# One list of 19 places for weight pieces and their parts, a new order of the last experts, and a reordered tail, in a one-core decoder layer

## The chip, the cores and the metric

The kernel runs on one core of a Trainium2 chip. The metric is the device time of one execution in microseconds (us). A profiled execution also gives a span, from the first to the last instruction; all times of single instructions below come from that execution.

## The reference, cut to what matters

One decoder layer over 512 tokens of width 1024, in f32: a mixer (retention heads beside sliding-window attention), then a mixture of experts, then an embedding gate and a last norm.

```python
h = h + jnp.concatenate([ret, att], axis=-1) @ w_out[i]
h = h + moe(rmsnorm(h, g_moe_norm[i]), w_router[i], b_router[i],
            w_up[i], b_up[i], w_down[i], b_down[i])        # top 4 of 32 experts
gate = jax.nn.sigmoid(h @ w_ple_gate[i])
h = h + rmsnorm(gate * (p[i] @ w_ple_proj[i]), g_ple_norm[i])
...
return rmsnorm(h, g_final)
...
def expert_block(args):
    xblk, e = args
    h = xblk @ w_up[e] + b_up[e]                           # 1024 x 2048
    return clamped_swiglu(h) @ w_down[e] + b_down[e]       # 1024 x 1024
```

Every expert's weights are read once: 12 MB for each of 32 experts.

## The kernel before

**Stages.** The mixer runs first and ends with the out-projection (`w_out`, in four pieces) and the routing. Then the 32 experts run one after the other, and last the tail: the projection of `p` by `w_ple_proj`, the gate product `h @ w_ple_gate` for four tiles of 128 tokens (`gate`, twice 512 columns for each tile), two norms, and the output.

**Pieces.** All weights come in pieces of 1 MB, a tile of 128 x 2048 f32 named `raw`. An expert has eight pieces for its up product (`w_up_piece`, L186) and four for its down product (`w_down_piece`, L192): 384 pieces, numbered here from 0 in the order in which SyncE (SP) issues them: up of expert 0, up of 1, down of 0, up of 2, down of 1, and so on. A piece can be issued when a place is free: there are RAW1 + RAW2 + RAW3 = 3 + 5 + 4 = 12 places in one ring, so the load of piece n waits for whatever empties the place of piece n - 12. SP's queue is in order; a load that waits holds all behind it.

**Large and small experts.** Experts are sorted by their count of tokens into 18 large ones ("L", up to 96 tokens) and 14 small ones ("S", up to 64), and `BIG` says which place in the sequence takes which kind. For an L expert every piece is split into a high part `wh` by ScalarE (ACT, L150) and a low part `wl`, the rest, by VectorE (DVE, L151); these have rings of their own, three deep each. TensorE (PE) then makes three products for each block (`wh` by the high rows, `wh` by the low rows, `wl` by the high rows; L847 for up, L928 for down). The raw place is free when the split is done. An S expert uses the raw piece itself (L864), with two matmuls in the array beside each other, and holds the place until PE is done.

**Order on PE.** In code, step e of the loop makes the up product of e, then the transposes of the rows of expert e + 1 (`prep` L300 or `prep64` L815), then the down product of e - 1. A scheduler turns this into one queue for each engine; `tc.issue_after` holds a step behind another. The rows of an expert are gathered from memory by GpSimd (POOL), `xe<-xg`.

**The tail.** After the last expert, `p` is transposed, the four token tiles are projected (three ahead of, one behind, a conditional), then comes the conditional itself (L1118, L1119: a path for experts with more tokens than their slots, which isn't taken with this input), then `h2` is read back from `acc` (L1177), and the gates run tile by tile: transposes of tile i, gate products of tile i, norm of tile i.

Of the kernel before, what the change touches and what calls it, by code (L numbers as in the profile page):

```python
# [22 lines left out]
P = 128  # L23
# [13 lines left out]
RAW1, RAW2, RAW3 = 3, 5, 4  # L37
# [9 lines left out]
BIG = [c == "L" for c in "LL" + "SLSLSLSLSLSLSLL" + "SLSLSLSLSLSLLLS"]  # L47
# [48 lines left out]
def hymba_kernel(ctx, tc, x, p, positions, rel_bias_table, g_mix_norm, w_in, b_in, ret_norm_g,  # L96
# [27 lines left out]
    rawp = pool(ctx, "rawp", RAW1)  # L124
    whp = pool(ctx, "whp", 3)
    wlp = pool(ctx, "wlp", 3)
# [7 lines left out]
    R = SimpleNamespace(eid={})  # L134
    free = [rawp] * RAW1

    def raw_tile(dt=F32):
        pl_ = free.pop(0)
        return pl_.tile([P, 2048], dt, name="raw"), pl_
# [58 lines left out]

    pieces = [w_ret(0, 0), w_ret(0, 4), w_kv, w_half(w_in, 0, 2048), w_half(w_in, 4, 2048)]
# [6 lines left out]
    for e in range(1, E + 1):  # L206
        if e < E:
            pieces += [w_up_piece(e, k) for k in range(8)]
        pieces += [w_down_piece(e - 1, f) for f in range(4)]
    n_moe = len(pieces)  # L210
# [6 lines left out]
    def prefetch(after=None):  # L217
        if free and state["next"] < min(len(pieces), state["limit"]):
            t, pl_ = raw_tile()
# [3 lines left out]
            queue.append((t, pl_))  # L223
            state["next"] += 1

    def next_piece(parts=None, dst=None, more=True):
        t, pl_ = queue.pop(0)
        r = split(t, parts, dst)
        free.append(pl_)
# [3 lines left out]

    def whole_piece(use):

        t, pl_ = queue.pop(0)
        use(t)
        free.append(pl_)
        prefetch()
# [87 lines left out]
    raw3 = pool(ctx, "raw3", RAW3)  # L327
    mix = [raw3.tile([P, 2048], F32R, name="raw").rearrange("p (a k t) -> a p k t", a=2, k=KD) for _ in range(NT)]
# [6 lines left out]
    p1 = px.enter_context(ExitStack())  # L335
    actp = pool(p1, "actp")
# [9 lines left out]
    prefetch()  # L346
    nc.sync.dma_start(out=xts[1], in_=x_v[:, 1, :])
    prefetch()
# [267 lines left out]
    raw2 = pool(right, "raw2", RAW2, side="right")  # L616
    rt = pool(right, "rt", side="right")
    free += [raw2] * RAW2
# [11 lines left out]
    b_hi = whp.tile([P, 2048], F32R, name="wh")  # L630
# [647 lines left out]
```

## Time and profile before

| what | value |
|---|---|
| time, median of 3 runs | 1489.59 us (1488.67 to 1491.34) |
| the profiled execution's own time | 1492.54 us |
| its span | 1490.8 us |
| TensorE busy in the span | 1359.1 us (91%) |
| VectorE, ScalarE, GpSimd busy | 826.1, 680.5, 222.7 us |
| mean granted TensorE clock | 0.952 of full speed (2.4 GHz) |
| bytes moved by DMA | 462.47 MB, 310 GB/s over the span |

The profiled execution is 2.95 us longer than the median, and 1.74 us of its time lie outside the span. Busy shares over the whole span mix a mixer, an expert stage and a tail that have different limits, so the rows further down are taken by stage.

### The profile page before, as it was taken

How to read it: one execution, taken by the hardware profiler on the slowest of the kernel's cores; microseconds unless marked ns; L12 is line 12 of the kernel's file. 1: busy time of each engine (PE TensorE's matmuls, PEld its weight loads, DVE VectorE, ACT ScalarE, POOL GpSimd, SP SyncE). 2: the span in 40 equal slices, each digit the busy share in tenths (PEclk: the TensorE clock that was granted, in tenths of full speed). 3: DMA queues.
4: the chain of work that ended last, by engine and by line, in shares of the span. 5: the costliest groups of instructions: out<-in, count | busy, mean ns of one | idle time of the engine just before them, and what ended most of it. 6: DMA issues, size and time to landing. Idle time of an engine off the chain costs nothing. (4 is left out here: it accounts for less than half of the span.)

```text
span 1490.8 us, 16875 instructions
## 1 busy us (share of the span) xinstructions
PE 1359.1 (91%) x6090; PEld 912.4 (61%) x6091; DVE 826.1 (55%) x1012; ACT 680.5 (46%) x756; POOL 222.7 (15%) x238
## 2 busy tenths in 40 slices
PE   5998999778999999999999999999999999999885
PEld 4776777566666474656556657474655647675564
DVE  6635674777456273545537647363544627683356
ACT  5332543545446253434526536353443625573443
POOL 1213132465010000001000000000100000000023
PEclk9997999879999999999999999999999999999998
DMA  8431027678799999999999999999999999987521
GB/s 264 124 101 57 3 107 287 226 261 315 254 408 391 409 396 394 408 397 403 387 389 407 397 389 387 383 403 392 391 396 396 392 387 401 396 325 289 172 79 45
DMA packets 110427, 462.47 MB, mean 310 GB/s; under 512 B 10830, under 2 KB 29180, under 8 KB 77568
## 3 DMA queue, kind: packets, MB, share of 16 engines
q1 hardware_dynamic: 99584, 436.24, 74.6%
q0 software_dynamic: 10320, 24.52, 6.5%
q8 instruction: 49, 0.80, 0.2%
q10 hardware_dynamic: 432, 0.57, 0.1%
q14 instruction: 42, 0.34, 0.1%
HBM read 447.26 MB, written 18.73 MB: 313 GB/s over the span
## 5 line engine op out<-in xcount | busy, mean ns | idle before, releaser
L151 DVE TENSOR_TENSOR wl<-raw,wh 128x2048 fp32r<-128x2048 f32 (+2 forms) x243 | 530.5, 2223 | 154.1 <-ACT wh L150 150.6
L150 ACT ACTIVATE wh<-raw 128x2048 fp32r<-128x2048 f32 (+2 forms) x243 | 442.9, 1858 | 111.3 <-PE up L847 56.1
L864 PE MATMUL up<-raw,xTh 128*64 128x512 f32 x896 | 195.4, 594 | 0.0
L896 DVE TENSOR_SCALAR a<-up 128x512 f32<-128x512 f32 x50 | 32.9, 687 | 265.9 <-ACT sg L895 265.9
L847 PE MATMUL up<-wh,xTh 128*128 128x512 f32 x576 | 162.5, 404 | 9.2 <-ACT wh L150 7.8
L847 PE MATMUL up<-wl,xTh 128*128 128x512 f32 x576 | 160.7, 401 | 2.2 <-DVE wl L151 2.2
L895 ACT ACTIVATE sg<-up 128x512 f32<-128x512 f32 x50 | 27.9, 594 | 295.1 <-issue 158.5
L847 PE MATMUL up<-wh,xTl 128*128 128x512 f32 x576 | 160.7, 401 | 0.9 <-DVE xTl L292 0.9
L864 PEld LDWEIGHTS up<-raw,xTh 128*64 128x64 f32 x896 | 63.1, 137 | 124.6 <-issue 120.0
L847 PEld LDWEIGHTS up<-wh,xTh 128*128 128x128 f32 x576 | 108.5, 191 | 40.3 <-ACT wh L150 13.1
L847 PEld LDWEIGHTS up<-wl,xTh 128*128 128x128 f32 x576 | 108.8, 190 | 32.8 <-DVE wl L151 7.0
L847 PEld LDWEIGHTS up<-wh,xTl 128*128 128x128 f32 x576 | 109.7, 191 | 28.0 <-DVE xTl L292 1.6
L928 PE MATMUL dn<-wh,aTh 128*128 128x512 f32 x288 | 101.7, 437 | 23.8 <-ACT wh L150 23.8
L928 PE MATMUL dn<-wl,aTh 128*128 128x512 f32 x288 | 104.8, 449 | 15.0 <-DVE wl L151 15.0
L942 POOL DMA_INDIRECT acc<-y,slot_i x30 | 45.4, 1515 | 444.1 <-ACT y L937 435.6
L800 POOL DMA_INDIRECT xe<-xg,slot_i x30 | 31.9, 1062 | 485.9 <-PE dn L857 261.0
L864 PE MATMUL dn<-raw,aT 128*64 128x512 f32 x448 | 102.9, 598 | 0.0
L928 PE MATMUL dn<-wh,aTl 128*128 128x512 f32 x288 | 98.6, 426 | 0.0
L928 PEld LDWEIGHTS dn<-wh,aTh 128*128 128x128 f32 x288 | 60.4, 215 | 43.0 <-ACT wh L150 27.3
L928 PEld LDWEIGHTS dn<-wl,aTh 128*128 128x128 f32 x288 | 58.6, 212 | 34.5 <-DVE wl L151 22.3
L914 DVE SCALAR_TENSOR_TENSOR aTl<-tp,aTh 128x512 fp32r<-128x512 f32 x36 | 24.1, 689 | 90.1 <-ACT aTh L913 90.1
L928 PEld LDWEIGHTS dn<-wh,aTl 128*128 128x128 f32 x288 | 59.8, 207 | 15.0
(342 smaller groups left out, 1581.9 us busy)
## 6 DMA issues: line engine op xcount, KB each, us to landing
raw<-in_w_up_dram SPq DMA_DIRECT2D x256, 1024.0 KB, 17.9
raw<-in_w_down_dram SPq DMA_DIRECT2D x128, 1024.0 KB, 18.6
raw<-in_w_in_dram SPq DMA_DIRECT2D x32, 256.0 KB, 4.9
raw<-in_w_out_dram SPq DMA_DIRECT2D x4, 1024.0 KB, 5.3
raw<-in_w_ple_gate_dram SPq DMA_DIRECT2D x4, 1024.0 KB, 11.6
raw<-in_w_in_dram SPq DMA_DIRECT2D x3, 1024.0 KB, 5.6
xt<-in_x_dram SPq DMA_DIRECT2D x4, 512.0 KB, 6.5
h<-in_x_dram POOLq DMA_DIRECT2D x4, 512.0 KB, 7.6
```

The lines of the kernel that those rows point to most:

```text
L150: R.split_act = nc.scalar.activation(to(wh), src(raw), AF.Copy)
L151: R.split_dve = nc.vector.tensor_tensor(out=to(wl), in0=src(raw), in1=to(wh).bitcast(F32), op=ALU.subtract)
L800: return nc.gpsimd.indirect_dma_start(out=dst[0:n, 0:D // h], out_offset=None, in_=xg.rearrange("s (h d) -> (s h) d", h=h), in_offset=bass ...
L847: nc.tensor.matmul(h[n // 2][:, n % 2 * 512:n % 2 * 512 + 512], lhsT=a[:, k, :], rhs=w[:, n * 512:(n + 1) * 512], start=(k == 0 and a is x ...
L864: R.pair = nc.tensor.matmul(o[v * 64:v * 64 + 64, c:c + 512], lhsT=xT[:, k, :], rhs=w[:, v * n + c:v * n + c + 512], start=False, stop=las ...
L895: nc.scalar.activation(sg[:, cs], hv[:, :, 0], AF.Silu, scale=ALPHA)
L896: nc.vector.tensor_scalar(a[:, cs], hv[:, :, 1], LIMIT + 1.0, 1.0 - LIMIT, op0=ALU.min, op1=ALU.max)
L914: nc.vector.scalar_tensor_tensor(flat(l[:, g4, :]), in0=flat(t), scalar=1.0 / ALPHA, in1=flat(h[:, g4, :]).bitcast(F32), op0=ALU.mult, op1 ...
L928: m = nc.tensor.matmul(o[:, n * 512:(n + 1) * 512], lhsT=a[:, k, :], rhs=w[:, kk * 1024 + n * 512:kk * 1024 + (n + 1) * 512], start=False, ...
L942: nc.gpsimd.indirect_dma_start(out=acc.rearrange("s (h d) -> (s h) d", h=h), out_offset=bass.IndirectOffsetOnAxis(ap=idx[0:n, :], axis=0), ...
```

## The change

It makes no other products; it changes where data lies and when steps are issued.

- **Places.** RAW2 becomes 9. The three-deep rings of `wh` and `wl` serve only the first stage; from the out-projection on, one list of 19 places (3 + 9 + 4 for pieces, and the 3 of `wh`) serves raw pieces and parts alike. `used()` gives the two places of a pair of parts back behind the products that read them; `room()` decides whether one more piece may be issued, so that a split always finds two places. `depth` is 2, and 3 from the experts on. The normed rows `xn` of the routing also take a place.
- **Sequence.** The last 15 experts go as SLSLSLLSLLSLLSS instead of SLSLSLSLSLSLLLS; the numbers of L and S are the same.
- **Transposes of expert 2.** They are written behind the down product of expert 0 (`turn`), where they were ahead of it; the others stay.
- **Tail.** The conditional path is written ahead of the last down product; the four token tiles are projected in one go; `w_ple_proj` is split in quarters; the transposes of tiles 0 and 1 come ahead of the first gate product, those of 2 and 3 ahead of the norms of 0 and 1; some products with `g_ple` and `g_fin` go from POOL to DVE; `mm` has 6 buffers instead of 4.

```diff
-RAW1, RAW2, RAW3 = 3, 5, 4
+RAW1, RAW2, RAW3 = 3, 9, 4
...
-BIG = [c == "L" for c in "LL" + "SLSLSLSLSLSLSLL" + "SLSLSLSLSLSLLLS"]
+BIG = [c == "L" for c in "LL" + "SLSLSLSLSLSLSLL" + "SLSLSLLSLLSLLSS"]
...
     def split(raw, parts=None, dst=None):
-        if dst is None:
-            wh = whp.tile([P, 2048], F32R, name="wh")
-            wl = wlp.tile([P, 2048], F32R, name="wl")
+        if dst is not None:
+            wh, wl = dst
+        elif R.wlp is not None:
...
         else:
-            wh, wl = dst
+            (wh, p0), (wl, p1_) = raw_tile(F32R, "wh"), raw_tile(F32R, "wl")
+            held.append((p0, p1_))
...
+    def room():
+
+        if R.wlp is not None:
+            return len(free) > 0
+        c = state["next"] - len(queue)
+        ahead = [j not in plain for j in range(c, min(c + R.depth, len(pieces)))]
+        return len(free) > 0 and len(free) + 2 * len(held) > 2 * sum(ahead) - (ahead.index(True) if any(ahead) else 0)
+
+    def prefetch(after=None, n=99):
+        while n and state["next"] < min(len(pieces), state["limit"]) and room():
...
+    def used():
+        free.extend(held.pop(0))
+        prefetch()
...
-            if e + 1 < E:
+            def turn():
+                return (prep if BIG[e + 1] else prep64)(xe[(e + 1) % 2])
+
+            if e + 1 < E and e != 1:
                 with tc.issue_after(R.up_end.ins):
-                    xT = (prep if BIG[e + 1] else prep64)(xe[(e + 1) % 2])
+                    xT = turn()
...
+            tf, tr = raw_tile(), raw_tile(F32R)
+            general_path(tf[0], tr[0])
+            R.up_end = R.rows_end = None
         if e > 0:
             big = BIG[e - 1]
             y = gated(down(aT, lambda f: next_piece(), e - 1) if big else down64(aT, e - 1), routes[e - 1][1])
             scatter(y, routes[e - 1][0], CAP if big else P, 1 if big else 2)
...
+        if e == 1:
+            xT = turn()
...
-    w_pr, *ws = [next_piece(more=False) for _ in range(3)]
+    quarters = [(lambda t, k=k: kslice(t, k), lambda t, k=k: kslice(t, k)) for k in range(4)]
+    w_pr = next_piece(quarters, more=False)
+    ws = [[next_piece(more=False) for _ in range(2)]]
...
     for j in (1, 2):
         project(up_tile(), (j,))
+    project(R.dn.tile([P, D], F32, name="dn"), (3,))
+    used()
     mx.close()
...
     transposed(0)
-    project(mm.tile([P, D], F32, name="dn"), (3,))
-    ws.append([next_piece(), next_piece(dst=(raw_tile(F32R)[0], raw_tile(F32R)[0]))])
+    transposed(1)
+    ws.append([next_piece() for _ in range(2)])
     gate(0, 0)
-    transposed(1)
     gate(1, 0)
     gate(0, 1)
+    transposed(2)
+    gate(1, 1)
     finish(0)
-    gate(1, 1)
+    transposed(3)
+    gate(2, 0)
     finish(1)
...
```

What SP issues from the last pieces of `w_out` to the first expert's work, before (`xg` and `acc` are the routing's writes):

```order
L156 DMA raw<-in_w_out_dram 128x4x512 x2
L186 DMA raw<-in_w_up_dram 128x2048 x3
L156 DMA raw<-in_w_out_dram 128x4x512 x2
L186 DMA raw<-in_w_up_dram 128x2048 x6
L775 DMA xg<-xn 128x1024
L776 DMA acc<-h_2064 128x1024
L186 DMA raw<-in_w_up_dram 128x2048
```

and after:

```order
L162 DMA raw<-in_w_out_dram 128x4x512
L192 DMA raw<-in_w_up_dram 128x2048
L162 DMA raw<-in_w_out_dram 128x4x512 x3
L192 DMA raw<-in_w_up_dram 128x2048 x10
L804 DMA xg<-xn 128x1024
L805 DMA acc<-h_2070 128x1024
L192 DMA raw<-in_w_up_dram 128x2048
```

Ahead of the routing's writes there are now 11 pieces of experts instead of 9 (four more follow between and behind those writes instead of three, before one waits for expert work), and three pieces of `w_out` instead of two stand behind the first expert piece.

What PE does between the up product of expert 1 and the down product of expert 0, before (`xe` are the gathered rows of expert 2):

```order
L847 MATMUL up<-wl,xTh 128x512 x4
L834 MATMUL up<-bias,sel 128x512 x4
L815 MATMUL tp<-cst,xe_2054 128x128 x4
L834 MATMUL dn<-bias,sel 128x512 x2
L928 MATMUL dn<-wh,aTh 128x512 x2
```

and after, first the same place, then the end of that down product:

```order
L881 MATMUL up<-wl,xTh 128x512 x4
L868 MATMUL up<-bias,sel 128x512 x4
L868 MATMUL dn<-bias,sel 128x512 x2
L966 MATMUL dn<-wh,aTh 128x512 x2
L966 MATMUL dn<-wh,aTl 128x512 x2
```

```order
L966 MATMUL dn<-wh,aTh 128x512 x2
L966 MATMUL dn<-wh,aTl 128x512 x2
L966 MATMUL dn<-wl,aTh 128x512 x2
L849 MATMUL tp<-cst,xe_2060 128x128 x4
L902 MATMUL up<-raw,xTh 64x512 x32
```

The four transposes of the rows `xe` moved behind the whole down product, next to the up product that needs them.

PE at the end of the experts, before (`raw` in the transposes is `p`; `wh,raw` are projections):

```order
L928 MATMUL dn<-wl,aTh 128x512 x2
L857 MATMUL dn<-bias,sel_9540 128x512
L864 MATMUL dn<-raw,aT_9428 64x512 x15
L300 MATMUL tp<-cst,raw 128x128 x4
L864 MATMUL dn<-raw,aT_9428 64x512
L300 MATMUL tp<-cst,raw 128x128 x4
L307 MATMUL dn<-wh,raw 128x512
```

and after:

```order
L895 MATMUL dn<-bias,sel_9492 128x512
L902 MATMUL dn<-raw,aT_9441 64x512 x12
L849 MATMUL tp<-cst,a 128x128 x4
L902 MATMUL dn<-raw,aT_9441 64x512 x4
L895 MATMUL dn<-bias,sel_10009 128x512
L902 MATMUL dn<-raw,aT_9516 64x512 x15
L325 MATMUL tp<-cst,raw 128x128 x4
L902 MATMUL dn<-raw,aT_9516 64x512
L325 MATMUL tp<-cst,raw 128x128 x4
L1083 TENSOR_LOAD any_blk
L1084 COMPARE_AND_BRANCH
```

The expert before the last one is now small (L902 with a raw piece), and the conditional's load and branch stand between the transposes of `p` and the projections.

## Rows read from the trace of the kernel before

**Rows 1.** Stretches: from:to, length, busy PE, PEld, DVE, ACT, POOL, granted clock, DMA share, GB/s.

```profile
212.00:385.00 173.00, 144.45 (x697) 112.14 (x697) 116.46 (x222) 82.52 (x97) 76.60 (x98) 0.91 0.70 256
385.00:1270.00 885.00, 840.65 (x3673) 523.86 (x3671) 455.54 (x302) 401.97 (x339) 69.99 (x54) 0.97 1.01 394
1270.00:1376.00 106.00, 99.77 (x437) 67.75 (x434) 68.24 (x47) 57.48 (x45) 5.01 (x4) 0.97 0.89 343
1376.00:1390.00 14.00, 13.51 (x52) 10.18 (x52) 8.99 (x4) 6.55 (x6) 0.00 (x0) 0.88 0.03 9
1390.00:1419.00 29.00, 23.86 (x98) 14.43 (x98) 8.40 (x8) 13.23 (x18) 2.98 (x2) 0.94 0.77 259
1419.00:1476.00 57.00, 51.82 (x240) 41.52 (x239) 34.82 (x81) 23.56 (x47) 16.47 (x13) 0.94 0.14 53
1476.00:1491.00 15.00, 0.00 (x0) 0.00 (x0) 7.97 (x24) 3.40 (x10) 4.25 (x5) 0.58 0.09 35
```

**Rows 2.** Timeline of SP's DMA issues: start, time from first to last, line, transfer, count.

```profile
385.40 9.45 SPq L186 DMA_DIRECT2D raw<-in_w_up_dram  x8
...
408.46 19.90 SPq L186 DMA_DIRECT2D raw<-in_w_up_dram  x8
...
1244.75 18.72 SPq L186 DMA_DIRECT2D raw<-in_w_up_dram  x8
...
1342.43 24.70 SPq L192 DMA_DIRECT2D raw<-in_w_down_dram  x8
```

**Rows 3.** The page's DMA issues: count, size, median us from issue to landing.

```profile
raw<-in_w_up_dram SPq DMA_DIRECT2D x256, 1024.0 KB, 17.9
```

**Rows 4.** Timeline of PE, experts 0 to 2: start, length, line, operation, [idle before <-releaser].

```profile
361.31 0.73 PE L834 MATMUL up<-bias,sel 64*128 64x512 f32 x4
367.60 1.09 PE L815 MATMUL tp<-cst,xe 128*128 128x128 f32 x4 [5.57 <-DMA xe<-xg,slot_i]
...
369.34 1.22 PE L928 MATMUL dn<-wh,aTh 128*128 128x512 f32 x2
...
383.43 13.95 PE L864 MATMUL up<-raw,xTh 128*64 128x512 f32 x64
```

**Rows 5.** The page's costliest groups, the two splits: busy, mean ns of one.

```profile
L151 DVE TENSOR_TENSOR wl<-raw,wh 128x2048 fp32r<-128x2048 f32 (+2 forms) x243 | 530.5, 2223 | 154.1 <-ACT wh L150 150.6
L150 ACT ACTIVATE wh<-raw 128x2048 fp32r<-128x2048 f32 (+2 forms) x243 | 442.9, 1858 | 111.3 <-PE up L847 56.1
```

**Rows 6.** Timeline of PE, one small and one large expert around 650 us.

```profile
654.24 0.73 PE L928 MATMUL dn<-wh,aTh 128*128 128x512 f32 x2 [2.16 <-ACT wh L150]
...
656.56 1.22 PE L928 MATMUL dn<-wl,aTh 128*128 128x512 f32 x2 [1.12 <-DVE wl L151]
...
658.43 1.05 PE L928 MATMUL dn<-wh,aTl 128*128 128x512 f32 x2
...
677.49 1.09 PE L847 MATMUL up<-wh,xTl 128*128 128x512 f32 x4
...
692.43 1.09 PE L847 MATMUL up<-wl,xTh 128*128 128x512 f32 x4
```

**Rows 7.** Timeline of PE, projections and first gate product.

```profile
1402.94 0.62 PE L307 MATMUL dn<-wh,raw 128*128 128x512 f32 x1 [2.54 <-ACT wh L150]
...
1414.15 0.50 PE L307 MATMUL dn<-wh,raw 128*128 128x512 f32 x1 [1.16 <-ACTq L1119]
...
1418.77 0.50 PE L307 MATMUL mm<-wh,hh 128*128 128x512 f32 x1 [0.73 <-ACT hh L291]
```

**Rows 8.** Timeline of PE, first gate products of token tile 2.

```profile
1446.65 0.73 PE L307 MATMUL mm<-wh,hh 128*128 128x512 f32 x2 [1.84 <-ACT hh L291]
1448.88 0.80 PE L308 MATMUL mm<-wh,hl 128*128 128x512 f32 x1 [1.50 <-DVE hl L292]
...
1451.18 0.63 PE L307 MATMUL mm<-wh,hh 128*128 128x512 f32 x1
...
1455.19 0.40 PE L309 MATMUL mm<-wl,hh 128*128 128x512 f32 x1
```

More of the change, by code (lines that the diff above doesn't have):

```diff
@@ L208, in hymba_kernel @@
             pieces += [w_up_piece(e, k) for k in range(8)]
+            if not BIG[e]:
+                plain.update(range(len(pieces) - 8, len(pieces)))
         pieces += [w_down_piece(e - 1, f) for f in range(4)]
+        if not BIG[e - 1]:
+            plain.update(range(len(pieces) - 4, len(pieces)))
     n_moe = len(pieces)
@@ L215, in hymba_kernel @@
     state = {"next": 0, "limit": n_first}
-    def prefetch(after=None):
-        if free and state["next"] < min(len(pieces), state["limit"]):
-            t, pl_ = raw_tile()
+    def room():
[6 more added lines that the diff above has]
+        while n and state["next"] < min(len(pieces), state["limit"]) and room():
+            t, place = raw_tile()
             if after is not None:
@@ L222, in prefetch, with next_piece @@
             pieces[state["next"]](t)
-            queue.append((t, pl_))
+            queue.append((t, place))
             state["next"] += 1
[L226 to L229, printed above, removed]
+            n -= 1
+    def next_piece(parts=None, more=True):
+        t, place = queue.pop(0)
+        r = split(t, parts)
+        free.append(place)
         if more:
@@ L232, in next_piece @@
         return r
+    def used():
+        free.extend(held.pop(0))
+        prefetch()
     def whole_piece(use):
-        t, pl_ = queue.pop(0)
+        t, place = queue.pop(0)
         use(t)
-        free.append(pl_)
+        free.append(place)
         prefetch()
@@ L613, in hymba_kernel @@
     p1.close()
-    raw2 = pool(right, "raw2", RAW2, side="right")
+    R.wlp = None
+    raw2 = pool(right, "raw2", side="right")
     rt = pool(right, "rt", side="right")
-    free += [raw2] * RAW2
+    free += [(raw2, f"b{j}") for j in range(RAW2)]
+    free += high[1:]
     b_raw, b_pool = raw_tile()
@@ L848, in up, with after @@
                                      rhs=w[:, n * 512:(n + 1) * 512], start=(k == 0 and a is xT[0] and w is wh), stop=False)
+            used()
         R.up_end = add_bias(h, e, 0, 1024, start=False, stop=True)
         return h
+    def after(m):
+        return tc.issue_after(m.ins) if m is not None else nullcontext()
     def bias64(o, e, c0):
@@ L876, in down64 @@
         o = R.dn.tile([P, D], F32, name="dn")[:, 0:512]
-        with tc.issue_after(R.up_end.ins), tc.issue_after(R.rows_end.ins):
+        with after(R.up_end), after(R.rows_end):
             bias64(o, e, 1024)
@@ L1180, in hymba_kernel @@
             prefetch()
-    g_ple = bcast(ep2, g_ple_norm[0], D, "g_ple", nc.sync)
-    g_fin = bcast(ep2, g_final, D, "g_fin", nc.sync)
-    ws = [ws]
-    free += [t[1] for t in (last, tmp, tf, tr)]
+    g_ple, g_fin = last[0][:, 0:D], last[0][:, D:2 * D]
+    for dst, src in ((g_ple, g_ple_norm[0]), (g_fin, g_final)):
+        nc.sync.dma_start(out=dst, in_=src.rearrange("(o n) -> o n", o=1).broadcast_to([P, D]))
+    free += [t[1] for t in (tmp, tf, tr)]
     hT = {}
@@ L1216, in finish @@
         ss = []
+        o = [ep2.tile([P, 512], F32, name="o", bufs=4) for _ in range(2)]
         for c in range(2):
```

202 lines of the change are left out of this document (103 added, 99 removed).

## The prediction

> **What bounds the kernel now.** I read it by stage, not by the busy shares of the whole span. First the stretches [rows 1]. Between 385 and 1270 us the DMA share is 1.01 at 394 GB/s: the weight stream is full, and TensorE, busy for 840.65 of 885 us, waits for it now and then. The stream is not full in two places: from 212 to 385 us (share 0.70, so 0.30 x 173 = 52 us unused) and from 1270 to 1376 us (share 0.89, about 12 us). From 1376 to 1390 us it stands at 0.03: the last expert weights have landed by 1376. What comes behind that is a chain on PE and its helpers: 43 us to the first gate product at 1418.77 [rows 7], 57 us of gates, 15 us of norm and output without a matmul [rows 1].
>
> Second the pace. SP issues piece 44 at 408.46 and piece 344 at 1244.75 [rows 2]: 836.3 / 300 = 2.79 us for a piece, 33.5 us for an expert. Third what PE would need alone. Sixteen up steps take 692.43 - 677.49 = 14.94 us [rows 6], so 0.93 us for a step of four matmuls, 0.47 for a down step of two, 2.8 us for a piece of an L expert. A pair of one S and one L expert gets 2 x 33.5 = 67.0 us from the stream. In it PE idles for 2.16 and 1.12 us at the start of the L down product and then runs some six steps at about 0.85 instead of 0.47 us, 2.3 us lost at the lower clock (1.05 us for two matmuls) [rows 6]. So PE alone needs 67.0 - 3.3 - 2.3 = 61.4 us, and has 5.6 us in hand per pair. More places can't make the full stream faster; what they can do is fill its gaps at either end.
>
> **The change part by part.** The sum is made against the profiled execution, 1492.54 us, which is 2.95 us above the median of the runs.
>
> *Places, start.* Before, piece 32 is the first of the group at 385.40 [rows 2], from where the stream is full. After, the order has 15 pieces out before one waits for expert work, where it had 12, and each later load waits for PE to be done with the piece 15 (among L) to 19 (among S) before it. *Transposes of expert 2* remove the 5.57 us for which PE stands from 362 on for gathered rows [rows 4]: the down product of expert 0 follows the bias at once. It started at 369.34 after transposes and bias; now at about 362.7, without a low-clock start (its first rows are 1.22 us for two matmuls [rows 4], some 1.3 us lost in all), and the transposes cost their 1.1 us behind it, by when the rows are there (they landed at 367.6). Up of expert 2 so starts at about 376.4 instead of 383.43, 7 us earlier, and by then 20 pieces are used and 35 issued instead of 32: 3 x 2.79 = 8.4 us more. Together 15. Bounds: 0, if the new loads only lie idle longer, to 7 + 7 x 2.79 = 26 with a distance of 19. I take **-15**, since those first experts are L.
>
> *Depth of the parts.* What this costs is no row of before, where each part has three places. With one list, the splits run one or two pieces ahead. A split takes 1.86 us on ACT, then 2.22 on DVE [rows 5]. I follow an L run (four down and eight up pieces of 2.8 us, all landed) by the waits in the order: the second down piece waits 1.2 us for its low part, since that split may start only when the first piece's high part is used up; the last up piece waits 0.9 and 0.35 us, since its high part needs a place which the piece before it holds. In all 2.5 us per L expert, in gaps as short as the 1.16 us of [rows 7]. It fits into the 5.6 us in hand: 0 on the path. Bounds: 0 to two exposed splits, below.
>
> *Sequence of the last experts.* Three L in a row need 3 x 2.8 x 12 us of PE, about what the stream delivers in, with places full: the last load goes out at 1342.43 + 24.70 = 1367.1 [rows 2], 122 us behind piece 344, where 39 x 2.79 = 109 would do. Part of these 13 us is made up for by the shorter way when the stream is thin (17.9 us from issue to landing in the middle [rows 3], some 9 at the end: 1376 - 1367). So between 4 and 12 us; no gain at all is the other bound, if PE is what is late. I take **-6**. The last weights then land at 1376 - 21 = 1355.
>
> *Tail up to the gates.* Before: 43 us from landing to gate, with an L down product (24 x 0.47 = 11.2 us) and an S one behind the last landing, since PE was late by then. After, both last experts are S, and with the stream as the limit PE uses each piece as it lands; only the last quarter of the last down product and the transposes of `p` are left (some 4 us). `w_ple_proj` follows the last piece through the queue (0.5 MB of `p` and 1 MB, 4 us), its first quarter is split in about 1 us, PE projects from about 8 us behind the landing, instead of 27 (1402.94 - 1376 [rows 7]): 19 us. The projections and first transposes took 1418.77 - 1402.94 = 15.8 us and stay: the gap of 1.16 us goes, a second tile's transposes (1 us) come. **-19**. The branch stands ahead of the last scatter on ACT and POOL, and SP issues three gate pieces ahead of the reads of `h2` that it had ahead of two of them: the reads queue behind 3 x 2.6 us of transfers and the last scatter. That lies beside the projections; with the cover gone it costs up to 8 us, at best the term is -22.
>
> *Gates.* 57 us hold 5.2 us without a matmul [rows 1] and, behind the gaps of 1.84 and 1.50 us, a dozen matmuls at 0.63 instead of 0.40 us [rows 8], 2.4 us. Transposes ahead of norms remove most: **-7**, bounds 0 and -7.6. *End.* POOL's products go to DVE, which then has 0.7 us more in its chain but no engine beside it: **-1**, bounds +1 and -2. *Third piece of `w_out` later* (behind the mixer's last products): the first 36 products use the other half and hide its transfer; bare, it would cost up to 8 us in the unfilled stretch. 0. Smaller buffers for `sg` and `y`: 0, their users are in order already.
>
> Sum: -15 - 6 - 19 - 7 - 1 = -48; 1492.54 - 48 = 1444.5, less the 2.95 us: **1441.6**, say 1441.
>
> **The rivals.** (A) *The start gives nothing*: the stream is full at 385 us either way and the three pieces only wait in their places. For it: in this stretch the share also falls where the queue isn't blocked by places but by routing. Against: the idle 5.57 us is plainly a wait that the new order drops. 1441 + 15 = 1456. (B) *The branch costs a transfer.* Each engine stands at the conditional until its next instructions are there, now beside the full stream: 17.9 us [rows 3] instead of the 1.16 us that PE stood at it before [rows 7]. About 17 us on the path: 1458. Against: by that place the expert weights have just landed. (The Trainium skill, "Runtime: NRT & Kernel Launch", section "Instruction fetch mechanics", says that a taken branch out of the fetched pages makes the engine fetch by DMA before it goes on, an argument against moving it next to traffic. The trace agrees only with a small stall: 1.16 us, in a stretch with share 0.77 [rows 1].) (C) *The parts are too shallow*, ending slower: one exposed split costs 3.3 + 2.3 = 5.6 us [rows 6], just what PE has in hand. If two are exposed in every L expert, 16 of them lose 11.2 - 5.6 = 5.6 us each, 90 us: 1441 + 90 = 1531. It decides from 5.6 + 48 / 16 = 8.6 us of stall per L expert, about one and a half splits; then the gain is gone. For it: PE's reserve is small. Against: the waits counted above are 2.5 us, and the pieces themselves lie further ahead. (D) *All terms at their good end*: 26 + 12 + 22 + 7.6 + 2 = 70, 1420.
>
> **How the numbers follow.** Forecast, between 1430 and 1450: 0.56. A 0.15, B 0.12, D or nearer to it than to the forecast 0.08, C 0.06, and 0.03 for gains eaten up to within 0.2% of now, which is about what a measurement of this kernel can tell from no change. Faster 0.91, same 0.03, slower 0.06. Range: down to 1422, near D; up to 1466, which holds A and B and half of each on top of the other. It leaves out C and the worst sums.
>
> **What would show it.** The start: up of expert 2 near 376 us, the stream's share above 0.95 from there, no idle of 5 us at 362. The middle: waits of the L products for `wh` and `wl` of some 2.5 us per expert, share 1.0. The end: last weights near 1355, no stretch under 0.9 before. The tail: first gate product some 24 us later, gates in 50 us. The forecast is wrong if the share in the middle falls below 0.97 with PE's idle time put down to `wh` and `wl` (C), if the first gate product comes more than 35 us behind the last weight (B), or if the last weight lands later than 1365 (A).

## The result: 3.1% slower, and the profile after

The changed kernel takes 1538.24 us (1537.02 to 1541.03, four runs), the kernel before 1490.46 us on the same chip (1488.67 to 1498.98, four runs): a ratio of 1.0314, interval 1.0286 to 1.0342. The forecast was 1441, so the sign is wrong; nearest to the result comes rival C, which had a chance of 0.06. The profiled execution has a span of 1535.8 us against 1490.8.

The stretch of the experts in the kernel after, cut as in [rows 1]: from:to, length, busy PE, PEld, DVE, ACT, POOL, granted clock, DMA share, GB/s.

```profile
385.00:1270.00 885.00, 821.29 (x3536) 510.11 (x3536) 467.98 (x303) 411.80 (x336) 70.03 (x51) 0.97 0.98 376
```

The row has turned round. Before, the share was 1.01 at 394 GB/s with 3673 matmuls; now it is 0.98 at 376 GB/s with 3536. TensorE is no longer kept waiting by the stream; it is late itself, and the stream waits for places. The page of the profile says the same of the landing of a piece, which took 17.9 us before [rows 3]:

```profile
raw<-in_w_up_dram SPq DMA_DIRECT2D x256, 1024.0 KB, 11.2
```

A shorter landing is no faster memory: fewer pieces are out at a time. By rate times landing, an estimate, 376 GB/s x 11.2 us = 4.2 MB are under way, where it was 394 x 17.9 = 7.1 MB.

Where the time went is read best from the start of each up product in PE's timeline. "Slot" is the expert's place in the sequence, counted from 0; the first up product listed is slot 0, slot 1 is expert 2 of the text ahead (experts 0 and 1 run into one another). The last column is what lies between the last up product listed (slot 30) and the end of the span. All are us, and "pair" is the time for one S and one L expert.

| kernel | slot 0 | slot 1 | pair, slots 6 to 14 | slots 2 to 30 | slot 30 to end | span |
|---|---|---|---|---|---|---|
| before | 306.9 | 383.4 | 66.5 | 949.2 | 131.2 | 1490.8 |
| after | 325.8 | 394.9 | 68.6 | 985.4 | 124.6 | 1535.8 |
| gathers first | 306.6 | 376.5 | 68.6 | 984.7 | 124.7 | 1516.6 |
| gathers first, one split first | 311.6 | 381.4 | 63.5 | 932.7 | 125.9 | 1470.8 |
| the same, own rings | 302.0 | 373.5 | 65.9 | 922.8 | 125.3 | 1450.4 |

The first two rows give the loss: 18.9 us before the experts, 7.4 us won back by slot 1, 3.9 us lost from slot 1 to slot 2, 36.2 us among the later experts, 6.6 us won in the tail, 45.0 in all. Set against the terms of the forecast, that is +15.4 us for the start (forecast -15), +36.2 for the experts (depth 0 and sequence -6), -0.6 up to the first gate product (-19) and -6.0 behind it (-8). What the other rows are follows below.

**The start.** GpSimd's queue around 300 us, of the kernel before (start, length, engine, line, operation, count, [idle before it, and what ended it]):

```profile
296.76 2.81 POOL L800 DMA_INDIRECT xe<-xg,idx  x1 [0.85 <-DVE idx L795]
...
309.07 1.05 POOL L995 DMA_INDIRECT slot_d<-pay,dest  x1 [7.25 <-DVE dest L992]
```

and of the kernel after:

```profile
310.49 1.12 POOL L1034 DMA_INDIRECT slot_d<-pay,dest  x1 [8.12 <-DVE dest L1031]
...
318.78 0.97 POOL L1034 DMA_INDIRECT slot_d<-pay,dest  x1 [0.31 <-issue]
320.05 1.01 POOL L834 DMA_INDIRECT xe<-xg,idx  x1 [0.30 <-issue]
```

Before, the first rows are gathered as soon as their index is there. After, six scatters of the routing table stand ahead of that gather in the queue; the first of them waits 8.12 us for `dest`, and the gather goes out at 320.05. PE shows what that costs:

```profile
324.00 1.97 PE L325 MATMUL tp<-cst,xe 128*128 128x128 f32 x8 [16.02 <-DMA xe<-xg,idx]
```

**The experts.** What PE waits for, summed over the run (engine, line, releaser: us, times, longest), before:

```profile
PE dn L928 <- ACT wh L150: 23.8, 11, 2.2
PE dn L928 <- DVE wl L151: 15.0, 15, 1.2
...
PE up L847 <- ACT wh L150: 7.8, 13, 2.8
...
PE up L847 <- DVE wl L151: 2.2, 11, 0.2
```

and after:

```profile
PE up L881 <- ACT wh L156: 29.0, 26, 2.5
PE dn L966 <- ACT wh L156: 21.9, 11, 2.1
PE dn L966 <- DVE wl L157: 16.4, 18, 1.5
...
PE up L881 <- DVE wl L157: 4.5, 23, 0.2
```

Two kinds of wait are to be seen. Those of the down product are there in both kernels, alike in number and size. Those of the up product have grown from 7.8 + 2.2 = 10.0 to 29.0 + 4.5 = 33.5 us. One pair of the kernel after, on PE:

```profile
604.58 0.73 PE L966 MATMUL dn<-wh,aTh 128*128 128x512 f32 x2 [2.10 <-ACT wh L156]
...
606.91 1.19 PE L966 MATMUL dn<-wl,aTh 128*128 128x512 f32 x2 [1.13 <-DVE wl L157]
...
607.90 1.06 PE L966 MATMUL dn<-wh,aTh 128*128 128x512 f32 x2
...
623.88 1.20 PE L881 MATMUL up<-wh,xTh 128*128 128x512 f32 x4 [0.58 <-ACT wh L156]
...
642.40 1.19 PE L881 MATMUL up<-wh,xTh 128*128 128x512 f32 x4 [1.08 <-ACT wh L156]
```

and on ACT beside it:

```profile
601.12 0.60 ACT L933 ACTIVATE sg<-up 128x512 f32<-128x512 f32 x1 [13.47 <-issue]
601.65 1.09 ACT L316 ACTIVATE xTh<-tp 128x512 fp32r<-128x512 f32 x2
602.62 1.91 ACT L156 ACTIVATE wh<-raw 128x2048 fp32r<-128x2048 f32 x1
...
640.43 1.91 ACT L156 ACTIVATE wh<-raw 128x2048 fp32r<-128x2048 f32 x1 [2.72 <-PE up L881]
```

The first wait of PE (2.10 us) ends with the split that ACT begins at 602.62. ACT has stood idle for 13.47 us before that, at `sg`, the silu of the small expert, whose up product was still running on PE; the split stands behind `sg` and `xTh` in its queue. I call this the **front stall**: 2.10 and 1.13 us, and then the products at the lower clock (1.06 us for two), as in [rows 6]. The stretch behind it, with the granted clock third from the end:

```profile
607.00:612.00 5.00, 4.53 (x12) 3.28 (x12) 2.10 (x1) 3.17 (x2) 0.00 (x0) 0.66 1.01 323
```

The changed kernel holds the comparison in itself. Up to slot 5 the same ACT steps stand the other way round, though the code is one loop:

```profile
535.87 1.91 ACT L156 ACTIVATE wh<-raw 128x2048 fp32r<-128x2048 f32 x1 [11.71 <-PE up L902]
537.69 0.58 ACT L933 ACTIVATE sg<-up 128x512 f32<-128x512 f32 x1
```

There the split is ahead of `sg`, the down product starts without waiting for it, and a pair takes 63.5 us (slots 2 to 6). From slot 7 on the split is behind `sg`, there are ten front stalls, and a pair takes 68.6 us (slots 6 to 14).

The last wait of PE shown (1.08 us) belongs to a split that ACT begins only when PE has used up an earlier part (2.72 us, released by PE's up product): the **shared places**. (The Trainium skill, "PSUM — Partial Sum Buffer", section "Engine vs sequencer instructions", says that the queues of ScalarE, VectorE and GpSimd are strictly first in, first out. The trace agrees: a split stood behind `sg` while ACT was idle for 13.47 us, and a gather behind a scatter that waited 8.12 us. How much of the 13.47 us the split could have used, these rows don't say; in slot 5 it starts 1.8 us ahead of `sg`.)

**The tail.** PE and ACT of the kernel after, from the last down product to the first gate product:

```profile
1447.57 0.66 PE L325 MATMUL tp<-cst,raw 128*128 128x128 f32 x4
1453.38 0.73 PE L332 MATMUL dn<-wh,raw 128*128 128x512 f32 x1 [5.16 <-ACT wh L156]
...
1469.77 0.49 PE L332 MATMUL mm<-wh,hh 128*128 128x512 f32 x1 [2.53 <-ACT hh L316]
```

```profile
1452.12 0.69 ACT L976 ACTIVATE y<-dn,slots 128x512 f32<-128x512 f32 x1 [3.42 <-PEq L1084]
1452.71 3.98 ACT L156 ACTIVATE wh<-raw 128x512 fp32r<-128x512 f32 x5
```

From the start of the last up product to the first gate product it is 1469.77 - 1411.2 = 58.6 us, and was 1418.77 - 1359.6 = 59.2 [rows 7]: nothing gained. From there to the end of the span it is 66.0 us instead of 72.0.

### The profile page after: what moved, and what is told of

It reads as the page before. It is cut to its first block, busy times and chain, and to the rows that moved or that the text cites. A ratio compares the mean times of both kernels' runs of the same rounds, so it can differ in the third digit from the quotient of the medians.

```text
span 1535.8 us, 16954 instructions
## 1 busy us (share of the span) xinstructions
PE 1373.4 (89%) x6090; PEld 906.1 (59%) x6091; DVE 831.5 (54%) x1022; ACT 687.2 (45%) x759; POOL 206.4 (13%) x227
## 5 line engine op out<-in xcount | busy, mean ns | idle before, releaser
L157 DVE TENSOR_TENSOR wl<-raw,wh 128x2048 fp32r<-128x2048 f32 (+2 forms) x247 | 536.6, 2200 | 276.8 <-ACT wh L156 235.2
L156 ACT ACTIVATE wh<-raw 128x2048 fp32r<-128x2048 f32 (+2 forms) x247 | 450.3, 1838 | 267.0 <-PE up L881 80.6
L902 PE MATMUL up<-raw,xTh 128*64 128x512 f32 x896 | 204.5, 599 | 0.7 <-ACT xTh L850 0.7
L902 PEld LDWEIGHTS up<-raw,xTh 128*64 128x64 f32 x896 | 64.1, 138 | 127.6 <-issue 125.8
L966 PE MATMUL dn<-wh,aTh 128*128 128x512 f32 x288 | 101.5, 436 | 21.9 <-ACT wh L156 21.9
L834 POOL DMA_INDIRECT xe<-xg,slot_i x30 | 37.1, 1238 | 527.6 <-PE dn L895 262.0
L902 PE MATMUL dn<-raw,aT 128*64 128x512 f32 x448 | 100.5, 596 | 0.0
L966 PEld LDWEIGHTS dn<-wl,aTh 128*128 128x128 f32 x288 | 55.3, 208 | 45.6 <-DVE wl L157 34.4
L976 ACT ACTIVATE y<-dn,slots 128x1024 f32<-128x1024 f32 (+1 forms) x30 | 27.5, 917 | 119.0 <-PE dn L902 68.9
## 6 DMA issues: line engine op xcount, KB each, us to landing
raw<-in_w_up_dram SPq DMA_DIRECT2D x256, 1024.0 KB, 11.2
```

The costliest lines, as they stand in the source:

```text
L156: R.split_act = nc.scalar.activation(to(wh), src(raw), AF.Copy)
L157: R.split_dve = nc.vector.tensor_tensor(out=to(wl), in0=src(raw), in1=to(wh).bitcast(F32), op=ALU.subtract)
L834: return nc.gpsimd.indirect_dma_start(out=dst[0:n, 0:D // h], out_offset=None, in_=xg.rearrange("s (h d) -> (s h) d", h=h), in_offset=bass ...
L902: R.pair = nc.tensor.matmul(o[v * 64:v * 64 + 64, c:c + 512], lhsT=xT[:, k, :], rhs=w[:, v * n + c:v * n + c + 512], start=False, stop=las ...
L966: m = nc.tensor.matmul(o[:, n * 512:(n + 1) * 512], lhsT=a[:, k, :], rhs=w[:, kk * 1024 + n * 512:kk * 1024 + (n + 1) * 512], start=False, ...
L976: nc.scalar.activation(y[:, 0:o.shape[1]], o, AF.Copy, scale=gate)
```

## The experiments

Theory **Q** (queues): two instructions stand in front of others that could run, the scatters on POOL and the silu on ACT. Theory **P** (places): the shared places alone make PE late. Theory **S** (stream): the expert stage is bound by the stream, as I had it. Times are held against the kernel before of the same chip, 1490.2 to 1491.4 us.

### Gathers ahead of the scatters

```
+    with tc.issue_after(R.last_pool.ins):
         for i in range(NT):
             for k in range(4):
                 nc.gpsimd.indirect_dma_start(out=slot_d[k], ...
```

> The changed kernel, with the sixteen small scatters of the routing (slot_d) held behind the two gathers of the first experts' rows in GpSimd's queue. Theory (the delay at the start is the order of GpSimd's queue: the gather went out at 320.05, 15.6 us after its indices were there, behind six scatters and their wait): up of expert 0 starts some 13 to 16 us earlier than 325.8, at 310 to 313, and the whole is 1538 - 14 = 1524, if nothing later absorbs it. Rival (the delay is of the DMA queues, full of 15 preloaded pieces: the gather's own landing is late): the start stays at 320 or later and the time at 1535 to 1540.

1519.85 us, ratio 1.0186 [1.0137, 1.0236], so 18.4 us of the loss gone. POOL now:

```profile
298.76 1.11 POOL L834 DMA_INDIRECT xe<-xg,idx  x1 [1.87 <-DVE kc L1009]
```

Slot 1 starts at 376.5, and every later up product 18.3 to 19.4 us earlier than in the changed kernel. The shift stays the same through all experts, so nothing behind the start takes it back. That alone doesn't decide between P and S: the loads behind the first 15 pieces wait for PE too, so a stream would have moved with it.

Some 5 us of the shift are not the edit's. In this one profiled execution the mixer ran at a higher clock (last section); three later runs with the same order of GpSimd and the lower clock start slot 0 at 310.7 to 311.6, so 14 to 15 us ahead of 325.8. The order of the scatters cost 14 to 18 us.

### Parts back in rings of their own

```
-RAW1, RAW2, RAW3 = 3, 9, 4
+RAW1, RAW2, RAW3 = 3, 6, 4
...
+    wlp_ = pool(ctx, "wlp", 3)
...
-    R.wlp = None
...
-    free += high[1:]
```

> The changed kernel with the parts in rings of their own, three deep each as before, and 13 places for raw pieces (19 in all, as many as in the changed kernel); sequence, transposes and tail as in the changed kernel. Theory (the middle loses because parts and pieces share places: a split waits for a product two pieces back or one back): the large up product falls from 25.7 to about 23.5 us, a pair of one small and one large expert from 69.1 back to about 67 us, and the middle's loss of 40 us to 10 or less; time 1500 to 1510. Rival (the middle loses by the sequence or by the stream itself): the pair stays at 69 and the time above 1525.

1483.19 us, 0.9942 [0.991, 0.9973]. A pair is back at 66.6 us and slots 2 to 30 at 952.0, nearly what the kernel before needs (949.2). That is 33 of the 55 us that this run gains. Another 24 us lie ahead of slot 0 (301.7 instead of 325.8): the scheduler put the gathers ahead of the scatters by itself here, though the edit doesn't touch them, which the expectation of 1500 to 1510 did not have:

```profile
294.62 1.14 POOL L834 DMA_INDIRECT xe<-xg,idx  x1 [0.86 <-DVE ig L827]
```

P looked proved by this run, but the front stall is still in it (2.10 and 1.12 us), and it does not show whether the places cost that much by themselves, or only on top of the front stall.

### The old sequence in the changed kernel, the new one in the kernel before

```
-BIG = [c == "L" for c in "LL" + "SLSLSLSLSLSLSLL" + "SLSLSLLSLLSLLSS"]
+BIG = [c == "L" for c in "LL" + "SLSLSLSLSLSLSLL" + "SLSLSLSLSLSLLLS"]
```

> The changed kernel with the old sequence of the last 15 experts (SLSLSLSLSLSLLLS). Theory (shared places cost most where large experts follow each other, 20 to 28 lost 26 us of the 40): the neighbouring large experts stand in one place instead of two, but three in a row, so the loss is moved, not removed: time within 10 us of 1538. Rival (the new sequence as such costs the 26 us): time 1512 to 1520.

> The kernel before, with only the new sequence of the last 15 experts. The prediction's term -6 (4 to 12), with a small expert ahead of the last one another -4 to -5 behind the last landing: 1480. With shared places the new sequence cost 16 us until the last up product, and 9 in time. Theory (two large experts in a row need more places than there are, whichever way they are shared): 1490 to 1497 here. Rival (only the shared places make it dear): 1478 to 1484.

1529.63 us in the first (8.6 us faster than the changed kernel; slots 2 to 30 take 15.8 us less, the tail 9.2 us more) and 1495.7 us in the second, ratio 1.0034 [1.0006, 1.0061]: slots 2 to 30 take 7.6 us more, the tail 4.5 us less. In both the new sequence is a loss among the experts.

### The turn of expert 2's transposes, alone

```
-            if e + 1 < E:
+            if e + 1 < E and e != 1:
...
+        if e == 1:
+            xT = (prep if BIG[2] else prep64)(xe[0])
```

> The kernel before, with only the transposes of expert 2 moved behind the down product of expert 0. The prediction's term: up of expert 2 starts 7 us earlier, at 376 instead of 383.4. In the changed kernel its lag fell from 18.9 to 11.4 us there, 7.5 us. Theory (the gain is kept where the stream sets the pace, since the loads go out earlier): time 1483. Rival (the stream was 12 places deep anyway, and takes the gain back): up of expert 2 earlier by 7, the middle unchanged, time 1490.

1489.55 us, 0.9968 [0.9948, 0.9988]. From slot 0 to slot 1 it is 75.1 us instead of 76.5; in the changed kernel 69.1. So 1.4 of the expected 7 us came, and the time is 0.3% lower. The wait of 5.57 us for the gathered rows is gone, and the down product follows the bias at once; but the transposes now stand right ahead of the up product, and PE waits ahead of them for `aTl`:

```profile
377.37 0.81 PE L815 MATMUL tp<-cst,xe 128*128 128x128 f32 x4 [3.14 <-DVE aTl L914]
```

and another 0.69 us behind them, for `xTh`. The up product itself then takes 16.8 us, where it took 13.95 (15.65 in the changed kernel).

### The splits ahead of the silu in the kernel before

```
+            if e > 0 and BIG[e - 1] and not BIG[e]:
+                pre = [next_piece() for _ in range(3)]
+                with tc.issue_after(R.split_act.ins), tc.issue_after(R.split_dve.ins):
+                    a = act(h)
...
```

> The kernel before, with the first three splits of a large down product put ahead of the activation of the small expert in ScalarE's and VectorE's queues. Theory (the stall of 2.16 + 1.12 us and the low clock behind it come from ScalarE standing at sg for 13.3 us with the splits queued behind, not from the stream): the stall goes; if PE is what sets the pace in the middle, the pair falls from 67.0 towards 61.4 and the time by up to 60 us; if the stream sets it as well, the pair stays at 66 to 67 and the time within 10 us of 1490. The prediction's reading (PE waits there for the stream) gives no change of the stall at all.

1488.43 us, 0.9982 [0.9954, 1.0009]: nothing. ACT shows why:

```profile
650.26 1.08 ACT L291 ACTIVATE xTh<-tp 128x512 fp32r<-128x512 f32 x2 [13.89 <-PE tp L300]
651.24 5.51 ACT L150 ACTIVATE wh<-raw 128x2048 fp32r<-128x2048 f32 x3
```

The silu is behind the splits now, but the copy of the next expert's transposes had been behind the silu and is now at the head, waiting just as long. So the next run holds both back (the transposes with `issue_after` in the same way):

> The kernel before, with the first three splits of a large down product put ahead of both the activation of the small expert (sg) and the copies of the next expert's transposed rows (xTh) on ScalarE. In the run with sg alone moved the stall stayed at 2.16 + 1.13 us, and xTh had taken the place of sg. Theory A (the stall is the order of ScalarE's queue, and the weight stream sets the pace of the middle): the stall at the start of the large down product goes, TensorE's idle time moves elsewhere, the pair stays at 66 to 67 us, time 1480 to 1492. Theory B (the stall is the order of the queue, and TensorE sets the pace): the pair falls to 61 to 63 us, time 1430 to 1450. The prediction's reading (the stall is the stream's data that isn't there): the stall stays.

1476.49 us, 0.9886 [0.985, 0.9921]. With one split in place of three:

> The kernel before with one split of the down product ahead of silu and transposed rows (three gave 1476.5). Theory 'the head of ScalarE's queue is the stall, not the data': the 2.16 us and 1.12 us at the start of the down product go, 1474 to 1480. Rival 'one split only moves the wait to the second piece': 1483 to 1491.

1476.14 us, 0.9891 [0.9839, 0.9943]. In this run ACT is

```profile
651.75 1.91 ACT L150 ACTIVATE wh<-raw 128x2048 fp32r<-128x2048 f32 x1 [15.39 <-DMA raw<-in_w_down_dram]
653.57 0.58 ACT L895 ACTIVATE sg<-up 128x512 f32<-128x512 f32 x1
```

and PE at the same place

```profile
653.71 0.73 PE L928 MATMUL dn<-wh,aTh 128*128 128x512 f32 x2 [1.17 <-ACT wh L150]
```

Now the split is released by the transfer itself: once the order on ACT is right, the stream is what PE waits for, and the pair stays at 66.7 us. Here S holds. Both paces, ACT's order and the stream, lay within 1 us of each other, and removing one of them gained only some 15 us, 10.2 of them in two slots (4.5 us in slot 5, 5.7 in slot 16), where, I take it, pieces lay in reserve.

### One split ahead of the silu in the changed kernel

```
+            pre = []
+            if e > 0 and BIG[e - 1] and not BIG[e]:
+                pre = [next_piece() for _ in range(1)]
...
+            with c0, c1:
+                a = act(h)
...
-                with tc.issue_after(R.up_end.ins):
+                with tc.issue_after(R.up_end.ins), c0, c1:
```

> The changed kernel with gathers ahead of the scatters, and the first split of a large expert's down product put ahead of the silu of the small expert before it; parts still share the places. To be held against the same kernel without that (1519.85). Theory 'two causes add, the front stall by the order on ScalarE and the waits inside by the shared places': the 2.1 us wait at the head of each down product goes or shrinks by more than 1 us, and the pair falls by 2 to 4 us, 1480 to 1500, with the waits inside (up on wh 29 us in all) unchanged. Rival 'the shared places set the pace alone': a wait of the same size appears one piece later and the time stays within 5 us, 1515 to 1525.

1471.92 us, 0.9866 [0.9824, 0.9908], from 1519.85: 47.9 us for the place of one instruction per small expert behind a large one, more than was expected. Ten front stalls go with it, so some 5 us each. Nothing else differs from the run with gathers first; the places are shared as before. On ACT:

```profile
649.33 1.91 ACT L156 ACTIVATE wh<-raw 128x2048 fp32r<-128x2048 f32 x1 [11.71 <-PE up L902]
651.15 0.58 ACT L933 ACTIVATE sg<-up 128x512 f32<-128x512 f32 x1
651.62 1.09 ACT L316 ACTIVATE xTh<-tp 128x512 fp32r<-128x512 f32 x2
```

What PE waits for falls:

```profile
PE up L881 <- ACT wh L156: 24.5, 18, 2.5
PE dn L966 <- DVE wl L157: 20.1, 15, 1.5
...
PE up L881 <- DVE wl L157: 3.4, 17, 0.2
```

and the down products themselves get shorter. The page's groups with gathers first alone (count | busy us, mean ns of one | idle before):

```profile
L966 PE MATMUL dn<-wh,aTh 128*128 128x512 f32 x288 | 101.5, 436 | 21.9 <-ACT wh L156 21.9
L966 PE MATMUL dn<-wl,aTh 128*128 128x512 f32 x288 | 104.3, 446 | 17.0 <-DVE wl L157 16.8
L966 PE MATMUL dn<-wh,aTl 128*128 128x512 f32 x288 | 98.4, 425 | 0.0
```

and with the split ahead:

```profile
L966 PE MATMUL dn<-wl,aTh 128*128 128x512 f32 x288 | 95.5, 413 | 20.5 <-DVE wl L157 20.1
L966 PE MATMUL dn<-wh,aTh 128*128 128x512 f32 x288 | 94.1, 408 | 0.9 <-ACT wh L156 0.9
L966 PE MATMUL dn<-wh,aTl 128*128 128x512 f32 x288 | 90.4, 395 | 0.0
```

The waits for parts fall from 21.9 + 16.8 + 29.0 + 4.6 = 72.3 to 0.9 + 20.1 + 24.5 + 3.4 = 48.9 us, so by 23.4; the busy time of the same 864 down products from 304.2 to 280.0, so by 24.2. So about half of what the stalls cost was idle time, and half the lower clock behind them. A pair is 63.5 us in each of the six from slot 2 to slot 14, less than the 65.9 us that the stream needs for one (below): over these twelve experts PE used up a reserve.

### One split and own rings; three splits and own rings

Edits as above, put together.

> The changed kernel with gathers first, own three-deep rings for the parts, and one split ahead of the silu (the run with three stood at 1449.4; shared places with one split at 1471.9). Theory 'the shared places cost 2 us per pair of S and L and more in two L in a row, by themselves': with rings 1449 to 1456, experts of slots 2 to 30 in some 917 to 922 us instead of 932.6. Rival 'what the rings gave was the second and third split ahead': 1465 to 1475.

1453.31 us, 0.9744 [0.9695, 0.9793]. Against shared places it is 18.6 us: that is what they cost by themselves, with the queue's order cured. Half of it lies ahead of the experts (slot 0 at 302.0 instead of 311.6) and half among slots 2 to 30 (922.8 instead of 932.7 us). The pair takes 60.2 us from slot 2 to slot 6, where pieces lie ready, so shared places cost 63.5 - 60.2 = 3.3 us per pair; from slot 6 on it is 65.9 us, the stream's pace (share 1.02 at 400 GB/s between 385 and 800 us). So in the changed kernel Q and P both hold and add up, and S takes over when both are cured.

> The changed kernel with rings of their own for the parts and 13 raw places, the gathers ahead of the routing's scatters, and the first three splits of a large down product ahead of sg and xTh on ScalarE where a small expert stands between. If the stream sets the pace with rings (theory A of the run beside this): the stall goes, the time stays at 1478 to 1484. If TensorE does: 1440 to 1460.

1449.44 us, 0.9705 [0.9668, 0.9742], 3.9 us less than with one split; the pair takes 58.9 us from slot 2 to slot 6 and 66.0 from slot 6 on.

### More places kept for parts

```
-        R.depth = 3
+        R.depth = 6
```

> The changed kernel with gathers ahead of the scatters, and six of the 19 places kept for parts ahead of a run of large pieces instead of three; the pieces lie three fewer ahead. To be held against the same kernel with three (1519.85). Theory 'the wait is for a free place': the waits for high and low parts at the ends of the L products (0.2 to 1.1 us each, 2.8 us per large expert) fall by half or more, pair of S and L down from 68.6 to about 67, 1490 to 1505; up waits for wh below 15 us. Theory 'a list in one order binds whatever its depth', since a part takes the place that was freed earliest and waits for its own last user: nothing moves by more than 5 us, 1515 to 1525.

1511.9 us, 1.0139 [1.0096, 1.0182], 8 us less than with three (1519.85), and between what the two theories expected: slots 2 to 30 take 974.0 us instead of 984.7. The front stall stays (24.5 us, 13 times, on the down product), the up product's waits for `wh` fall from 29.0 to 21.8 us. What exactly binds the parts inside an L run is not settled by it.

### The old sequence and the branch, in the cured kernel

Both against the kernel with rings and three splits (1449.44 us).

> The kernel with own three-deep rings for the parts, gathers first and three splits ahead of the silu, but with the old sequence of the last experts (..SLSLSLSLLLS). Theory 'the new sequence is a loss': with the stream full until the last load (share 1.01 in the run before), LL pairs need 5.6 us of PE each that the stream can't give back; seven of the eight us lost in slots 20 to 30 in the kernel of before with the new sequence come back, and the tail, which now ends with an L down product, costs some 5 us more than with S: between 1440 and 1447, start of up in slot 30 at 1315 to 1318. Theory 'the sequence only hurts where PE is late': with splits ahead the new sequence is worth what the diff wants, and the old one gives 1452 to 1458.

1458.6 us, 0.9779 [0.9737, 0.982]: here the old sequence is the slower one by 9.2 us (8.3 among slots 2 to 30). The same edit that lost in the kernel before gains once PE isn't late.

> The same kernel with own rings, gathers first and splits ahead of the silu, with the crowded experts' path put back behind the projections, where the kernel of before has it. Theory 'the branch ahead of the last products costs': ScalarE stood 3.42 us at the branch with y of the last expert behind it, and the first projection waited 5.16 us for a part where it waited 2.54 before: 2 to 4 us faster, 1445 to 1447. Theory 'it hides beside the products there': the branch then stands on the path between the projections and the gates, with 1.2 to 3.4 us: 1449 to 1453.

1440.71 us (1440.1 to 1442.27), 0.9661 [0.962, 0.9703], the fastest of all, and more than was expected. Of its 8.7 us, some 4 lie ahead of the experts (slot 0 at 298.6 instead of 303.1, in the clock, last section); the rest is in the tail. PE there:

```profile
1354.33 0.66 PE L327 MATMUL tp<-cst,raw 128*128 128x128 f32 x4
1356.30 0.50 PE L334 MATMUL dn<-wh,raw 128*128 128x512 f32 x1 [1.31 <-ACT wh L157]
...
1373.03 0.80 PE L334 MATMUL mm<-wh,hh 128*128 128x512 f32 x1 [0.17 <-ACT hh L318]
```

From the last transposes to the first projection it is 2.0 us instead of 6.0 (1358.39 to 1364.40 in the kernel without this edit; 5.8 in the changed kernel). The same edit on the kernel with shared places and one split:

> The changed kernel with gathers first, one split ahead of the silu, shared places, and the conditional path behind the projections. Theory 'the branch costs about 5 us on ScalarE wherever it stands ahead of y': 1465 to 1469 (1471.9 without). Rival 'that was a gain by the earlier start of that run': 1470 to 1474.

1465.78 us, 0.9818 [0.9769, 0.9866], 6.1 us less than without it, with slot 30 at the same time to 0.1 us (1345.0 and 1344.9). From slot 30 to the end it is 119.5 instead of 125.9 us, and 119.9 instead of 124.4 in the pair of runs above. So the branch ahead of the last products costs 4 to 6 us.

## Why the prediction was wrong, point by point

**What bounds the kernel** is the step that failed first. The share of 1.01 and PE's idle time in [rows 6] were read as PE waiting for the stream with 5.6 us in hand per pair. The idle time was counted as reserve without asking who stood in front of the split that ended it. It was ACT's own queue, in the kernel before too:

```profile
650.71 0.60 ACT L895 ACTIVATE sg<-up 128x512 f32<-128x512 f32 x1 [13.30 <-issue]
651.30 1.08 ACT L291 ACTIVATE xTh<-tp 128x512 fp32r<-128x512 f32 x2
652.27 5.51 ACT L150 ACTIVATE wh<-raw 128x2048 fp32r<-128x2048 f32 x3
```

PE's pure need was about right (61.4 us worked out; 60.2 measured with own rings and one split ahead, 58.9 with three). But 60.2 plus the 5.6 us of front stall is 65.8 us, the stream's pace is 65.9, and the pair took 66.5. So there were two limits side by side, and next to nothing in hand; a stall that comes from the order of a queue stays when the stream gives way.

**Depth of the parts, 0.** The waits inside an L run were worked out at 2.5 us per L expert; shared places cost 3.3 us per pair. The size was near, the mechanism right; that they fit into the reserve was the error. With the front stall, 63.5 + 5.1 = 68.6 us makes a pair slower than the stream; without it, 63.5 is faster than the stream. The up product of a second L in a row waits 2.54 us, which is no price of shared places: it is 2.76 us in the kernel before and 2.75 with own rings. It comes four times in the changed kernel and twice in the kernel before, so by the sequence. Rival C had the right place and the wrong make-up: it asked for one and a half exposed splits per L expert; one was exposed already.

**Start, -15.** What was not read is POOL's queue. The prediction looked at PE, ACT and SP; the order that the scheduler gave to the scatters cost 14 to 18 us. The step on the transposes came out in number, and in part by luck: slots 0 to 1 take 69.1 us instead of 76.5, 7.4 us where 7 were forecast. Of these, 3.2 us are idle time of PE (8.9 us before, 5.7 after) and 4.2 are busy time, with the granted clock at 0.99 instead of 0.91: the first ten us of slot 0 were granted 0.63 before and 0.94 after. Alone, in the kernel before, the turn gave 1.4 us, because the transposes and their waits moved onto the path, which the step had at 1.1 us. From slot 1 to slot 2 the changed kernel then lost 3.9 us again. The 8 us of three more pieces never showed: with the gathers cured slot 2 starts at 407.2 to 412.4 with shared places and at 402.3 with own rings and one split ahead, where it was 410.4.

**Sequence, -6.** It gave +8.6 us in the changed kernel and +5 in the kernel before, but -9.2 in the kernel with rings and splits first. The working (the last loads earlier) was right under its condition, a stream that sets the pace, which the front stall took away.

**Tail, -19.** Measured -0.6, from the start of the last up product to the first gate product. The term supposed that PE would use each piece as it lands. In fact the last weights landed near 1420 us (the share is 0.87 from 1410 to 1420 and 0.18 in the next 10 us), PE then had the rest of the last up product and two down products to do, and it reached the projection at 1453.38. And the branch, costed at nothing beside the products, cost 4 to 6 us: ACT stood 3.42 us until PE's sequencer came to line 1084, with `y` and all splits for the projection behind it. Rival B had the place right and the price (17 us) too high. (It cited the Trainium skill, "Runtime: NRT & Kernel Launch", "Instruction fetch mechanics", on a fetch at a taken branch. The row of 3.42 us names PE's sequencer as the releaser, as the 1.16 us in [rows 7] names ACT's, which I read as engines meeting at the branch; a fetch of its own is not to be seen here.)

**Gates and end, -8.** Measured -6.0, from 72.0 to 66.0 us: right within its bounds.

**The signs to look for.** The share was to fall below 0.97 in the middle if C came true; it read 0.98 with 36 us lost among the experts. The rate was the better sign: it fell from 394 to 376 GB/s, by 4.6%, the share by 3%. The other two signs came true, but not for the rivals that they were meant for: the last weights landed near 1420 us (A had 1365 as its limit), and the first gate product came some 50 us behind them (B had 35). Both say that PE is late, and neither says why.

## What to carry to other kernels

Before idle time is called reserve, look at the engine that ends it: if that engine was idle too, with "issue" or another engine's product ahead of the awaited instruction in its queue, the wait is one of order, stays when the other limit is lifted, and can be removed by one move (here 48 us in the changed kernel, 15 in the kernel before). When a scheduler decides the order, compare all queues around a change, GpSimd's above all, since here a scatter that waited held up the gather behind it. Compare them along one kernel and between variants too: the split changed its place between slots 5 and 7 of one loop, and the gathers moved by themselves in the run with own rings. And an edit's sign depends on which limit is last: the new sequence lost 5 to 9 us while TensorE was late and gained 9 when it wasn't.

## What the runs showed of the chip beyond that

- **The front stalls cost about twice the idle time that they added.** Behind gaps of 2.10 and 1.13 us, two down matmuls took 1.06 us instead of 0.63, and the granted clock of the five us behind the gaps was 0.66, a mixture of 2.4 and 1.2 GHz. Behind a single gap of 1.45 us, in the run with one split first, they stayed at 0.62 and the clock at 1.00 (650 to 660 us). The 24.2 us of busy time above fit that, beside 23.4 us of idle time.
- **The mixer differs by 5 us in the same code.** From 140 to 170 us, ahead of everything that the edits concern, the granted clock was 0.88 to 0.92 in nine of eleven profiled executions of the changed kernel and its variants, and 1.00 in two (gathers first; branch behind the projections), which reach slot 0 some 4 to 5 us sooner than kernels with the same order there. Comparisons of single spans hold that uncertainty: between "gathers first" and "one split first", slots 2 to 30 alone give 52 us, the medians 47.9.
